# Written order for VectorE and ScalarE in attention, and the later modulation rows summed on VectorE

## Chip, cores and metric

One core of one Trainium2 chip. The metric is the time of one execution of the program on the device, in microseconds (us): the median of three runs before the change. Times of single instructions and waits come from one profiled execution. TensorE does the matrix products and the transposes (into PSUM), VectorE, ScalarE and GpSimd the elementwise work, SyncE issues the DMA loads and stores.

## What is computed

One layer of a diffusion backbone over 1024 latent tokens of width 1024, with 256 context tokens. Cut to what matters here (`mod` is one product of a 1024-vector with a 1024 x 6144 matrix, which gives six rows of 1024):

```python
mod = jax.nn.silu(c) @ w_ada + b_ada
sh1, sc1, gt1, sh2, sc2, gt2 = jnp.split(mod, 6, axis=-1)
h = modulate(rmsnorm(x, g_mix), sh1, sc1)          # h * (1 + scale) + shift
q, k, v, bg, cg, hv = jnp.split(h @ w_in, SPLIT_POINTS, axis=-1)
att = windowed_attention(rope(q), rope(k), v, k_c, v_c, sink)   # 8 heads of 64, window of 128
conv = bg * conv3(cg * hv)                          # depthwise, 3 taps
x = x + gt1 * (jnp.concatenate([att, conv], -1) @ w_out)
h2 = modulate(rmsnorm(x, g_ffn), sh2, sc2)
x = x + gt2 * expert_choice_ffn(h2, w_router, w_gate, w_up, w_down)   # 16 experts
return rmsnorm(x, g_final)
```

The softmax of a query runs over a sink, the 256 context keys and the latent keys within 128 positions. The inputs are float32; every large operand is split into a high and a low half in a reduced format, and a product is three products of halves.

## The kernel before, in words

The work is staged. First come sh1 and sc1 by themselves (to 37.9 us), since everything else needs them. Then x and ctx are normed, transposed, modulated and split into hT, and the keys and values are projected (`build_hT`, `proj_kv`, driven by `kv_stream`, to 90.8). `q_stream` projects eight query tiles of 128 tokens (`q_proj`: 24 matmuls of 512 columns, rotary on VectorE at L327 to L334, the split into halves at L509 and L510; `q_turn` transposes them, L520). Beside both runs `mod_stream`: the other four modulation rows. For each it loads 8 pieces of 512 KB (L460), ScalarE scales a piece by silu(c) (L461) and GpSimd adds it (L463); a small product with 0/1 columns sums over the partitions (L473), the bias is added (L489) and the rows go to DRAM (`rows_d`), from where later stages fetch them. A function `weave` draws from both generators in proportion to given totals, which sets the order in which instructions are written; `urgent` gives the projection's a higher priority with the scheduler.

Attention is 32 units, eight blocks of 128 queries times four head pairs. `scores(u)` makes the two score blocks of a pair on TensorE (L563, L565), adds the mask and takes the row maximum (L575), negates and scales it (L577), and has ScalarE form the exponentials with their sums (L578). Two additions and an exponential of the sink complete the sum (L585 to L587), a reciprocal follows (L588), and the blocks are scaled by it, one on ScalarE (L592), one on VectorE (L594). `values(u)` transposes the probabilities (L622) in three groups, ScalarE casts each group to its high half (L625), VectorE subtracts for the low half (L626, here called pth), TensorE forms the value products (L613), and the two parts are joined into attT (L639, L643). In the loop of `attention` the scores of unit u and the values of unit u-1 alternate, and `weave` mixes in `conv`: 12 weight tiles (`wcs`: loaded, cast on ScalarE at L710, low half on GpSimd at L711), each 16 steps of three matmuls (L730 to L732). After every third tile's partner the three taps of the conv are applied: GpSimd at L755 and L760, ScalarE at L759. `prepare` and what follows it loads the output projection's weights in four parts, multiplies them by gt1 (L776) and splits them (L223, L224). Then `project` runs over the token tiles with the router and the sort, and the experts follow.

Only TensorE runs in written order (`manual_schedule`); the other engines' instructions are put in order by a scheduler. Large tiles come from 21 slots, small ones from rings of three buffers (`w4`, `wm`).

## Time and profile before

| | us |
|---|---|
| runs of the kernel, median (lowest to highest) | 1165.14 (1164.18 to 1167.07) |
| profiled execution, its own time | 1163.48 |
| its span | 1161.7 |
| busy: TensorE, VectorE, ScalarE, GpSimd | 1058.4, 967.2, 766.1, 351.0 |
| to the end of sh1 and sc1 | 37.9 |
| hT, keys and values | 37.9 to 90.8 |
| queries | 90.8 to 178.5 |
| attention and conv | 178.5 to 433.5 |
| output projection, router, sort | 433.5 to 576.4 |
| experts | 576.4 to 1126.0 |
| last rows out | 1126.0 to 1161.7 |

The stretches are cut where the first instruction of the next stage's kind starts on TensorE. Busy time is the time in which an engine executes instructions; matmuls overlap in the engine's pipeline, so a busy TensorE need not be at its peak. In a row of waits the engine and line on the left had nothing to do until the one on the right finished.

### The profile page before, as it was taken

Reading aid. Unit: us, or ns where it says so; the run is one execution under the profiler, and the core shown is the slowest. Engines: PE = TensorE matmul, PEld = TensorE weight load, DVE = VectorE, ACT = ScalarE, POOL = GpSimd, SP = SyncE. Lnnn points to the kernel's source line nnn. Section 1 sums busy time; section 2 is a strip of 40 time slices with the busy share of each in tenths; the row PEclk is TensorE's granted clock in tenths of the full one; section 3 lists DMA queues with packets and bytes.
Section 4 is the critical chain, followed back from the end, with each engine's and each line's share of the span. In section 5 each row is a group of like instructions: output and inputs, shape, how many; then the busy total and the mean of one; then the engine's idle time right before and its main releaser. Section 6 shows DMA issues by size and latency. Waiting matters only on the chain.

```text
span 1161.7 us, 15615 instructions
## 1 busy us (share of the span) xinstructions
PE 1058.4 (91%) x5486; PEld 873.5 (75%) x5486; DVE 967.2 (83%) x1661; ACT 766.1 (66%) x1058; POOL 351.0 (30%) x292
## 2 busy tenths in 40 slices
PE   6786889999899998999399999999999999999981
PEld 2675667888788877888288888888888888888861
DVE  7888455887878785389899999999999999999975
ACT  7565655767666643232288878878878877888853
POOL 0457681221303031222212433322333322330022
PEclk9897999999999999999599999999999999999996
DMA  9644440010101079648789999999999999999555
GB/s 376 232 164 144 164 146 19 24 33 1 55 1 37 19 278 339 181 127 270 273 322 356 399 403 390 391 388 389 395 404 392 389 389 389 394 404 390 203 195 221
DMA packets 90790, 292.89 MB, mean 252 GB/s; under 512 B 7044, under 2 KB 20816, under 8 KB 89688
## 3 DMA queue, kind: packets, MB, share of 16 engines
q1 hardware_dynamic: 84808, 270.40, 61.0%
q0 software_dynamic: 5904, 21.50, 7.7%
q8 instruction: 43, 0.70, 0.2%
q14 instruction: 35, 0.29, 0.1%
HBM read 266.69 MB, written 25.18 MB: 251 GB/s over the span
## 4 chain that ended last, share of the span: by engine, by line
PE 72%; DVE 13%; issue 5%; ACT 4%; DMA 4%; POOL 1%; POOLq 0%; ACTq 0%; DVEq 0%; SPq 0%
PE pg L1313 14%; PE pu L1313 14%; PE py L1313 13%; PE po L879 7%; PE ps_cv L731 3%; PE ps_cv L730 3%; PE ps_cv L732 3%; PE pt L622 2%; PE po_att L613 2%; DVE whl L1150 2%; PE ps_s L565 2%; PE xTp L1299 1%; PE ps_s L563 1%; PE pl L954 1%; PE hTtp L1299 1%
## 5 line engine op out<-in xcount | busy, mean ns | idle before, releaser
L1150 DVE TENSOR_TENSOR whl<-raw,whl 128x1024 fp32r<-128x1024 f32 x384 | 455.2, 1224 | 29.9 <-ACT whl L1147 18.9
L1147 ACT CAST whl<-raw 128x1024 fp32r<-128x1024 f32 x384 | 400.2, 1054 | 100.2 <-PE pu L1313 35.6
L1313 PE MATMUL pg<-whl,xT 128*128 128x512 f32 x768 | 186.2, 395 | 2.1 <-DVE whl L1150 2.1
L1313 PE MATMUL pu<-whl,xT 128*128 128x512 f32 x768 | 180.9, 392 | 0.0
L1313 PEld LDWEIGHTS pg<-whl,xT 128*128 128x128 f32 x768 | 142.3, 189 | 31.6 <-DVE whl L1150 2.9
L1313 PE MATMUL py<-whl,hTt 128*128 128x512 f32 x720 | 165.9, 389 | 0.0
L1313 PEld LDWEIGHTS pu<-whl,xT 128*128 128x128 f32 x768 | 143.0, 188 | 29.4
L1313 PEld LDWEIGHTS py<-whl,hTt 128*128 128x128 f32 x720 | 135.1, 188 | 28.4 <-DVE whl L1150 0.3
L1278 POOL TENSOR_SCALAR oh<-iota,pos 128x128 bf16<-128x128 f32 x104 | 100.5, 981 | 0.5
L1371 POOL DMA_INDIRECT acc_d<-yt,idx x15 | 38.5, 2565 | 196.0 <-DVE yt L1359 196.0
L1323 POOL DMA_INDIRECT xr<-h_d,idx x16 | 22.3, 1395 | 199.2 <-DVE gate_w L1289 199.2
L730 PE MATMUL ps_cv<-hTh,wcs 128*128 128x512 f32 x192 | 81.5, 424 | 0.0
L463 POOL TENSOR_TENSOR acc<-acc,wmod 128x1024 f32<-128x1024 f32 x28 | 70.0, 2518 | 27.8 <-ACT wmod L461 26.7
L625 ACT CAST pth<-pt 128x512 fp32r<-128x512 f32 (+1 forms) x88 | 46.1, 524 | 46.2 <-PE pt L622 46.1
L731 PE MATMUL ps_cv<-hTl,wcs 128*128 128x512 f32 x192 | 76.1, 397 | 0.0
L732 PE MATMUL ps_cv<-hTh,wcs 128*128 128x512 f32 x192 | 76.0, 396 | 0.0
L879 PE MATMUL po<-woh,ah 128*128 128x512 f32 x240 | 70.8, 404 | 0.6 <-ACT woh L223 0.6
L626 DVE TENSOR_TENSOR pth<-pt,pth 128x512 fp32r<-128x512 f32 (+1 forms) x88 | 53.9, 613 | 20.1 <-ACT pth L625 19.2
L711 POOL TENSOR_TENSOR wcs<-wcr,wcs 128x1024 fp32r<-128x1024 f32 x12 | 28.6, 2389 | 110.2 <-ACT wcs L710 87.5
L578 ACT ACTIVATE sm<-sm,negm 128x640 f32<-128x640 f32 (+1 forms) x64 | 51.6, 807 | 4.0 <-DVE negm L577 3.9
L575 DVE CUSTOM_DVE_ANT_0 sm<-ps_s,maskt,sink 128x640 f32<-128x640 f32 (+1 forms) x56 | 48.3, 863 | 6.9 <-PE ps_s L565 6.3
L879 PEld LDWEIGHTS po<-woh,ah 128*128 128x128 f32 x240 | 44.1, 191 | 9.4 <-ACT woh L223 1.0
(297 smaller groups left out, 1828.4 us busy)
## 6 DMA issues: line engine op xcount, KB each, us to landing
raw<-in_w_gate_dram SPq DMA_DIRECT2D x64, 1024.0 KB, 9.6
raw<-in_w_up_dram SPq DMA_DIRECT2D x64, 1024.0 KB, 7.8
raw<-in_w_down_dram SPq DMA_DIRECT2D x64, 1024.0 KB, 9.6
wmod<-in_w_ada_dram SPq DMA_DIRECT2D x32, 512.0 KB, 3.7
wa<-in_w_ada_dram SPq DMA_DIRECT2D x8, 1024.0 KB, 5.3
wcr<-in_w_in_dram SPq DMA_DIRECT2D x12, 512.0 KB, 3.8
xt<-in_x_dram SPq DMA_DIRECT2D x4, 1024.0 KB, 20.6
wor<-in_w_out_dram SPq DMA_DIRECT2D x4, 1024.0 KB
```

Of the source, the lines that this page charges most:

```text
L463: nc.gpsimd.tensor_tensor(acc, acc, wt, op=OP.add)
L575: nc.vector.tensor_tensor_reduce(dst, src, mk, op0=OP.add, op1=OP.max, scale=1.0, scalar=sink8[:, h:h + 1], accum_out=mx[:, b, h:h + 1])
L578: nc.scalar.activation(sm, sm, AF.Exp, bias=negm[:, b, h:h + 1], scale=0.125, accum_out=esum[:, b, h:h + 1])
L626: nc.vector.tensor_tensor(pth[:, 1, :n], pt[:, :n], pth[:, 0, :n].bitcast(F32), op=OP.subtract)
L730: mm(ps, wsp[:, 0, k], hi, start=k == 0, stop=False)
L731: mm(ps, wsp[:, 0, k], lo, start=False, stop=False)
L732: mm(ps, wsp[:, 1, k], hi, start=False, stop=k == KC - 1)
L879: mm(po[n], a, wo[k // 4, n][j][:, k % 4], start=first, stop=last)
L1147: nc.scalar.copy(w[:, 0], t[:, k % 2])
L1150: low = nc.vector.tensor_tensor(w[:, 1], t[:, k % 2], w[:, 0].bitcast(F32), op=OP.subtract)
L1278: nc.gpsimd.tensor_scalar(oh[:, t], iota1, pos[:, t, 0, e:e + 1], None, op0=OP.is_equal)
L1313: mm(ps[n], a_hl[:, a, k], w[:, j, n * 512:(n + 1) * 512], start=first, stop=last)
```

## The change

Six things, in the order of the program:

1. Small constants: all rows of `b_ada` and `g_ffn` are loaded and transposed with the others, so that a modulation row can be finished as a column (`modv`, 128 x 32).
2. `build_hT` gives all steps the same engines: ScalarE modulates, ScalarE casts, VectorE subtracts. The low half of the k/v weights goes from GpSimd to VectorE.
3. `mod_stream` and `urgent` go. Rows 1 and 2 (sh2, sc2) are summed on VectorE, one 128x1024 chunk of each per query tile, tied behind that tile's split (`mod_tile`); row 0 (gt1) is done in attention, one step a unit, in chunks of 384, 384 and 256 columns (`mod_attention`); row 3 (gt2) in 16 steps beside the projection of tiles 1 to 4 (`last_row`). Sums over partitions are small products with a column of ones.
4. The query halves are made with the factor -0.125, the masks are positive, and a minimum takes the maximum's place: it is then directly the bias of the exponential, which runs with scale -1 over one more column, that of the sink. The `negm` instructions and the sink's two additions and exponential go; a copy of two sink values a unit comes.
5. Attention and conv run in written order on VectorE and ScalarE too. The loop has six explicit places a unit; the join of a unit's values moves into the next unit; the second exponential has a place of its own.
6. Conv weights' low halves and the taps go from GpSimd to VectorE, in pieces of 512 columns at set steps; the first tap goes to ScalarE. Loading, gating and splitting of the output weights stand apart.

```diff
-        nc.gpsimd.tensor_tensor(wkv_l[:, ks], wkv_r[:, ks], wkv_h[:, ks].bitcast(F32), op=OP.subtract)
+        nc.vector.tensor_tensor(wkv_l[:, ks], wkv_r[:, ks], wkv_h[:, ks].bitcast(F32), op=OP.subtract)
...
-        if k % 2:
-            nc.scalar.activation(hf, ps[:, :n], AF.Identity, scale=mscale[:, k, j:j + 1], bias=mshift[:, k, j:j + 1])
-            nc.vector.tensor_copy(hi, hf)
-            nc.vector.tensor_tensor(lo, hf, hi.bitcast(F32), op=OP.subtract)
-        else:
-            nc.vector.tensor_scalar(hf, ps[:, :n], mscale[:, k, j:j + 1], mshift[:, k, j:j + 1],
-                                    op0=OP.mult, op1=OP.add)
-            nc.scalar.copy(hi, hf)
-            (nc.gpsimd if mem is None or k < 4 else nc.vector).tensor_tensor(lo, hf, hi.bitcast(F32), op=OP.subtract)
+        nc.scalar.activation(hf, ps[:, :n], AF.Identity, scale=mscale[:, k, j:j + 1], bias=mshift[:, k, j:j + 1])
+        nc.scalar.copy(hi, hf)
+        nc.vector.tensor_tensor(lo, hf, hi.bitcast(F32), op=OP.subtract)
...
-            nc.sync.dma_start(wt, wada_k[k][:, (2 + r) * D:(3 + r) * D])
-            nc.scalar.activation(wt if k else acc, wt, AF.Copy, scale=silu_c[:, k:k + 1])
-            if k:
-                nc.gpsimd.tensor_tensor(acc, acc, wt, op=OP.add)
...
+    def mod_add(src, k, acc, out=None):
+        if k == 0:
+            return nc.vector.tensor_scalar(acc, src, silu_c[:, 0:1], None, op0=OP.mult)
+        return nc.vector.scalar_tensor_tensor(acc if out is None else out, src, silu_c[:, k:k + 1], acc, op0=OP.mult,
+                                              op1=OP.add)
...
+    def mod_tile(t):
+        if t == 0:
+            macc.extend(slots.get((2, D), F32, "acc"))
+        st_ = [wm("wmod") for _ in range(2)]
+        for r in (1, 2):
+            mod_load(st_[r - 1], r, t, slice(0, D))
+        yield
+        for r in (1, 2):
+            add = mod_add(st_[r - 1], t, macc[0][:, r - 1])
+            tc.add_manual_dep(add.ins, q_split[-1].ins.name,
+                              mybir.DependencyInfo(mybir.DependencyClass.Sync, mybir.DependencyReason.DATA),
+                              reason="order")
...
+            w = cols[n].stop - cols[n].start
+            src = stage[:, i % 2, :w]
+            last = k == KC - 1
+            mod_add(src, k, accp[:, :w], src if last else None)
+            if last:
+                yield 1
+                mod_sums(accp, src, 0, cols[n].start // 128)
+            load(i + 2)
...
         qs = w4("qs", (8, 2, HD), F32R)
         tv = t1.rearrange("p (h d) -> p h d", d=HD)
-        nc.scalar.copy(qs[:, :, 0, :], tv)
-        nc.vector.tensor_tensor(qs[:, :, 1, :], tv, qs[:, :, 0, :].bitcast(F32), op=OP.subtract)
+        nc.scalar.activation(qs[:, :, 0, :], tv, AF.Copy, scale=-0.125)
+        low = nc.vector.scalar_tensor_tensor(qs[:, :, 1, :], tv, -0.125, qs[:, :, 0, :].bitcast(F32), op0=OP.mult,
+                                       op1=OP.subtract)
         qs_of[t] = qs
+        q_split.append(low)
+        for _ in mt:
+            pass
...
-    weave([(urgent(steps(kv_stream(), q_stream())), 95.0), (mod_stream(), 56.0)])
+    for _ in steps(kv_stream(), q_stream()):
+        pass
...
+        def exp(i):
+            h = 2 * hp + i
+            sx = sm2[:, i, :W + 1]
+            nc.scalar.activation(sx, sx, AF.Exp, bias=mx[:, b, h:h + 1], scale=-1.0,
+                                 accum_out=esum[:, b, h:h + 1])
...
             else:
                 mk = maskt[:, 0:W]
-            nc.vector.tensor_tensor_reduce(dst, src, mk, op0=OP.add, op1=OP.max, scale=1.0,
+            if i == 0:
+                nc.vector.tensor_copy(sm2[:, :, W], sink8[:, hs])
+                for f in joined[:1]:
+                    f(0)
+            nc.vector.tensor_tensor_reduce(dst, src, mk, op0=OP.add, op1=OP.min, scale=1.0,
                                            scalar=sink8[:, h:h + 1], accum_out=mx[:, b, h:h + 1])
-            nc.vector.tensor_scalar(negm[:, b, h:h + 1], mx[:, b, h:h + 1], -0.125, None, op0=OP.mult)
-            nc.scalar.activation(sm, sm, AF.Exp, bias=negm[:, b, h:h + 1], scale=0.125,
-                                 accum_out=esum[:, b, h:h + 1])
             if i == 0:
-                yield
-        hs = slice(2 * hp, 2 * hp + 2)
-        r = rec[:, b, hs]
-        nc.vector.tensor_tensor(r, sinkb[:, hs], negm[:, b, hs], op=OP.add)
-        nc.scalar.activation(r, r, AF.Exp)
-        nc.vector.tensor_tensor(r, r, esum[:, b, hs], op=OP.add)
-        nc.vector.reciprocal(r, r)
+                exp(0)
+                if joined:
+                    joined.pop()(1)
+            yield
+        exp(1)
+        yield
+        nc.vector.reciprocal(rec[:, b, hs], esum[:, b, hs])
...
-            for i, g in enumerate((sc, va, sc, va, va, va)):
-                next(g, None)
-                if i < 5:
-                    yield 1
-                if u == 0 and g is sc:
-                    yield 1
+            next(sc, None)
+            if u == 4 * NT:
+                joined[0](0)
+                joined.pop()(1)
+            if u and mrow is not None:
+                next(mrow, None)
+            yield 1
+            next(va, None)
+            yield 1
+            next(sc, None)
+            yield 1
+            next(va, None)
+            next(sc, None)
+            yield 1
+            if u == 0:
+                yield 1
+            next(va, None)
+            next(sc, None)
+            yield 1
+            next(va, None)
+        joined[0](0)
+        joined.pop()(1)
...
+    def conv_split(i, low, n):
+        if i < 12:
+            raw, wsp, _ = conv_w_of[i]
+            ks = slice(4 * n, 4 * n + 4)
+            if low:
+                nc.vector.tensor_tensor(wsp[:, 1, ks], raw[:, ks], wsp[:, 0, ks].bitcast(F32), op=OP.subtract)
+            else:
+                nc.scalar.copy(wsp[:, 0, ks], raw[:, ks])
...
+                    at = 8 * half + k
+                    if at in (7, 8, 9, 10):
+                        conv_split(i + 1, *divmod(at - 7, 2))
+                    if part == 2 and at < 4:
+                        j, n0 = 1 + at // 2, at % 2 * 512
+                        yt_ = st["y"][:, n0:n0 + 512]
+                        nc.vector.scalar_tensor_tensor(yt_, st["u"][:, j + n0:j + n0 + 512],
+                                                       convT_w[:, 4 * j + f:4 * j + f + 1], yt_, op0=OP.mult, op1=OP.add)
+                    if k < KC - 1:
+                        yield 1
...
-                nc.gpsimd.tensor_scalar(y, u[:, 0:S], convT_w[:, f:f + 1], None, op0=OP.mult)
-                tap = wm("tap", (S,))
-                for j in (1, 2):
-                    w = convT_w[:, 4 * j + f:4 * j + f + 1]
-                    nc.scalar.activation(tap, u[:, j:j + S], AF.Copy, scale=w)
-                    nc.gpsimd.tensor_tensor(y, y, tap, op=OP.add)
+                nc.scalar.activation(y, st["u"][:, 0:S], AF.Copy, scale=convT_w[:, f:f + 1])
                 st["y"] = y
...
-    weave([(steps(attention(), prepare()), 160.0), (conv(), 161.0)])
...
+    pb = p2(1, "po_att")
+    with tc.manual_schedule(engines={ET.PE, ET.DVE, ET.Activation}):
+        weave([(steps(attention(), prepare()), 152.0), (conv(), 161.0)])
...
+        yield 6
+        for i, (n, k) in enumerate(items):
+            mod_add(mem[:, 1 + i % 3], k, mem[:, 0])
+            load(i + 3)
+            if k == KC - 1:
+                yield 1
+                mod_sums(p1(1, "prow"), mem[:, 0], 3, 4 * n)
+            yield 1.8
+        mod_row(p1(1, "prow"), 3)
+        slots.put(s_)
```

Where it moves instructions, at three places. Names in the rows: t is a query tile under rotary, qs its halves, wmod a loaded piece of a modulation row, acc its sum; ISA is the masked minimum or maximum with its read-out (mx), pth a low half of transposed probabilities, wcr and wcs a conv weight and its halves, attT the joined values, stage and po_att the pieces and the running sum of the gt1 row.

VectorE, query stage, from the rotary of one tile to the start of the next, before:

```order
L327 TENSOR_TENSOR t_1281<-ps_q,ropet 128x512
L329 TENSOR_TENSOR t_1281<-ps_q,ropet 128x512
L333 TENSOR_TENSOR t_1281<-t_1281 128x8x32
L334 TENSOR_TENSOR t_1281<-t_1281 128x8x32
L510 TENSOR_TENSOR qs<-t_1281,qs 128x8x64
L327 TENSOR_TENSOR t_1340<-ps_q,ropet 128x512
L329 TENSOR_TENSOR t_1340<-ps_q,ropet 128x512
```

and with the change:

```order
L322 TENSOR_TENSOR t_1246<-ps_q,ropet 128x512
L324 TENSOR_TENSOR t_1246<-ps_q,ropet 128x512
L328 TENSOR_TENSOR t_1246<-t_1246 128x8x32
L329 TENSOR_TENSOR t_1246<-t_1246 128x8x32
L624 COPY sm_1321<-sink_282 128x2
L545 SCALAR_TENSOR_TENSOR qs<-t_1246,qs 128x8x64
L447 SCALAR_TENSOR_TENSOR acc_860<-wmod,silu_c,acc_860 128x1024 x2
L322 TENSOR_TENSOR t_1298<-ps_q,ropet 128x512
L324 TENSOR_TENSOR t_1298<-ps_q,ropet 128x512
```

The two chunks (L447 x2) now stand between a tile's split and the next tile's rotary.

VectorE, attention, a unit in which a conv weight is split, from the first pth of the values to the scaling of the scores, before:

```order
L626 TENSOR_TENSOR pth<-pt,pth 128x512
L575 ISA sm_2238,mx<-ps_s,maskt,sink_285 128x640
L575 ISA mx 128x1
L577 TENSOR_SCALAR negm<-mx 128x1
L585 TENSOR_TENSOR rec<-sinkb,negm 128x2
L626 TENSOR_TENSOR pth<-pt,pth 128x512
L587 TENSOR_TENSOR rec<-rec,esum 128x2
L588 RECIPROCAL rec<-rec 128x2
L626 TENSOR_TENSOR pth<-pt,pth 128x256
L594 TENSOR_SCALAR sm_2238<-sm_2238,rec 128x640
```

and with the change (from the join of the last unit's values on):

```order
L698 TENSOR_TENSOR attT_1487<-po_att,up 64x128 x2
L447 SCALAR_TENSOR_TENSOR po_att<-stage,silu_c,po_att 128x384
L828 TENSOR_TENSOR cg<-ps_cv,cg 128x512
L676 TENSOR_TENSOR pth<-pt,pth 128x512
L627 ISA sm_1840,mx<-ps_s,maskt,sink_282 128x640
L627 ISA mx 128x1
L781 TENSOR_TENSOR wcs_1750<-wcr,wcs_1750 128x512
L676 TENSOR_TENSOR pth<-pt,pth 128x512
L781 TENSOR_TENSOR wcs_1750<-wcr,wcs_1750 128x512
L676 TENSOR_TENSOR pth<-pt,pth 128x256
L636 RECIPROCAL rec<-esum 128x2
L642 TENSOR_SCALAR sm_1840<-sm_1840,rec 128x640
```

The L577, L585 and L587 rows are gone; the join, a chunk and two halves of a conv weight's low part (L781) stand among the rest, the first of them ahead of the second pth, the second ahead of the third.

VectorE, from the last query tile into attention, before:

```order
L327 TENSOR_TENSOR t_1386<-ps_q,ropet 128x512
L329 TENSOR_TENSOR t_1386<-ps_q,ropet 128x512
L333 TENSOR_TENSOR t_1386<-t_1386 128x8x32
L334 TENSOR_TENSOR t_1386<-t_1386 128x8x32
L855 MEMSET vals 128x512
L510 TENSOR_TENSOR qs<-t_1386,qs 128x8x64
L489 TENSOR_TENSOR bias<-mrows,bias 4x1024
L575 ISA sm_1404,mx<-ps_s,maskt,sink_285 128x512
L575 ISA mx 128x1
```

and with the change:

```order
L322 TENSOR_TENSOR t_1298<-ps_q,ropet 128x512
L324 TENSOR_TENSOR t_1298<-ps_q,ropet 128x512
L627 ISA sm_1321,mx<-ps_s,maskt,sink_282 128x512
L627 ISA mx 128x1
L328 TENSOR_TENSOR t_1298<-t_1298 128x8x32
L329 TENSOR_TENSOR t_1298<-t_1298 128x8x32
L545 SCALAR_TENSOR_TENSOR qs<-t_1298,qs 128x8x64
L781 TENSOR_TENSOR wcs_1313<-wcr,wcs_1313 128x512
L447 SCALAR_TENSOR_TENSOR acc_860<-wmod,silu_c,acc_860 128x1024 x2
L781 TENSOR_TENSOR wcs_1313<-wcr,wcs_1313 128x512
```

The bias of the rows is gone; the first minimum of attention stands ahead of the second half of the last rotary, and the first conv weight's low halves stand behind the last split, on either side of the last two chunks.

## Rows read from the trace of the kernel before

**Rows 1.** The table of stretches of the core, one row each (bounds in us from the start of the span, length, busy us of each engine with its number of instructions, granted TensorE clock as a share of full speed, share of the DMA engines, GB/s): the query stage, attention, and the output projection with the router.

```profile
90.80:178.50 87.70, 68.10 (x300) 50.44 (x298) 55.51 (x78) 46.60 (x65) 63.75 (x38) 0.92 0.47 150
178.50:433.50 255.00, 247.71 (x1465) 213.10 (x1466) 197.76 (x509) 164.93 (x345) 56.56 (x23) 0.99 0.15 50
433.50:576.40 142.90, 118.57 (x654) 99.87 (x652) 105.77 (x440) 43.09 (x91) 32.09 (x64) 0.91 0.74 238
```

**Rows 2.** Waits in the query stage (engine and line, what it waited for, us in total, times, longest us).

```profile
DVE t L327 <- PE ps_q L503: 24.6, 7, 6.0
PE pq L520 <- DVE qs L510: 13.1, 5, 4.6
```

**Rows 3.** All instructions of one line over the whole span (number, duration in ns as minimum/median/maximum, first and last start in us, forms): the split of a query tile, and the add of a softmax sum.

```profile
L510 DVE TENSOR_TENSOR qs<-t,qs x8: 691/692/2106, 113.6 to 176.6; 128x512 fp32r<-128x512 f32 x8
...
L587 DVE TENSOR_TENSOR rec<-rec,esum x32: 142/160/2326, 186.0 to 409.8; 128x2 f32<-128x2 f32 x32
```

**Rows 4.** Groups of instructions in the query stage (line, engine, operation, names, shapes, number | busy us, mean ns of one | idle time of the engine before them, and what ended it): GpSimd's additions of the modulation, and ScalarE's cast of a query tile.

```profile
L463 POOL TENSOR_TENSOR acc<-acc,wmod 128x1024 f32<-128x1024 f32 x24 | 59.5, 2496 | 25.7 <-ACT wmod L461 24.5 <-PE ps_q L503 0.5 <-ACT vx L343 0.5
...
L509 ACT CAST qs<-t 128x512 fp32r<-128x512 f32 x8 | 5.0, 622 | 18.9 <-DVE t L334 18.9
```

**Rows 5.** Groups in attention, the same columns; pth is a transposed probability block, sm a score block, rec the reciprocal sums, attT the joined output, wcs a split conv weight.

```profile
L626 DVE TENSOR_TENSOR pth<-pt,pth 128x512 fp32r<-128x512 f32 x64 | 44.1, 690 | 19.4 <-ACT pth L625 18.5
L575 DVE CUSTOM_DVE_ANT_0 sm<-ps_s,maskt,sink 128x640 f32<-128x640 f32 x48 | 42.4, 882 | 5.0 <-PE ps_s L565 4.4
...
L711 POOL TENSOR_TENSOR wcs<-wcr,wcs 128x1024 fp32r<-128x1024 f32 x10 | 23.9, 2392 | 107.9 <-ACT wcs L710 85.2 <-PE po_att L613 22.7
...
L643 DVE TENSOR_TENSOR attT<-po_att,up 64x128 f32<-64x128 f32 x64 | 18.1, 282 | 10.8 <-ACT up L639 10.4
...
L594 DVE TENSOR_SCALAR sm<-sm,rec 128x640 f32<-128x640 f32 x24 | 13.6, 568 | 0.2
...
L587 DVE TENSOR_TENSOR rec<-rec,esum 128x2 f32<-128x2 f32 x32 | 12.0, 376 | 5.2 <-ACT rec L586 4.5
...
L626 DVE TENSOR_TENSOR pth<-pt,pth 128x256 fp32r<-128x256 f32 x24 | 9.8, 409 | 0.7 <-ACT pth L625 0.7
...
L575 DVE DVE_READ_ACCUMULATOR2_ANT mx<- 128x1 f32 x64 | 5.3, 83 | 0.0
```

**Rows 6.** Time line of TensorE in the query stage (start us, us, engine, line, operation, names, shapes, number, and in brackets the idle time before it with what ended it): first and last of 24 products between two turns, a turn, the next product.

```profile
154.50 0.48 PE L501 MATMUL ps_q<-wqh,hTh 128*128 128x512 f32 x1
...
159.84 0.39 PE L503 MATMUL ps_q<-wqh,hTl 128*128 128x512 f32 x1
162.81 1.09 PE L520 MATMUL pq<-ident,qs 128*128 128x128 f32 x8 [2.59 <-DVE qs L510]
163.66 0.48 PE L501 MATMUL ps_q<-wqh,hTh 128*128 128x512 f32 x1
```

**Rows 7.** Groups in the k/v stage (columns as in rows 4): products with the low half of hT, GpSimd's low half, and ScalarE's modulation.

```profile
L318 PE MATMUL ps_kv<-wkvh,hTl 128*128 128x256 f32 x64 | 20.0, 312 | 4.8 <-POOL hTl L297 2.5 <-DVE hTl L292 2.3
...
L297 POOL TENSOR_TENSOR hTl<-hf,hTh 128x512 fp32r<-128x512 f32 x4 | 5.7, 1436 | 6.0 <-ACT hTh L296 6.0
...
L290 ACT ACTIVATE hfs<-ps_xt,mshift,mscale 128x512 f32<-128x512 f32 x4 | 3.1, 776 | 0.0
```

**Rows 8.** All instructions of a line (columns as in rows 3): two forms of VectorE that multiply by a scalar and combine with a second tensor, in later stages.

```profile
L933 DVE SCALAR_TENSOR_TENSOR h<-xres,rstd,rowsA x7: 1283/1285/1286, 453.9 to 536.6; 128x1024 f32<-128x1024 f32 x7
...
L1359 DVE SCALAR_TENSOR_TENSOR yt<-py,gate_w,GT x32: 739/744/752, 622.9 to 1145.8; 128x512 f32<-128x512 f32 x32
```

**Rows 9.** Time line between the query stage and attention (columns as in rows 6): the row sums of the modulation, and the first score products.

```profile
172.71 3.60 PE L473 MATMUL mrows<-acc,sel 128*4 128x512 f32 x8
...
178.47 0.73 PE L563 MATMUL ps_s<-kcv,qT 128*128 128x256 f32 x2 [2.16 <-DVE bias L489]
```

**Rows 10.** Time line in attention (columns as in rows 6): the first score product of four units, and one add of a softmax sum.

```profile
291.70 2.33 DVE L587 TENSOR_TENSOR rec<-rec,esum 128x2 f32<-128x2 f32 x1
...
292.06 0.40 PE L563 MATMUL ps_s<-kcv,qT 128*128 128x256 f32 x2
...
301.64 0.40 PE L563 MATMUL ps_s<-kcv,qT 128*128 128x256 f32 x2
...
308.59 0.40 PE L563 MATMUL ps_s<-kcv,qT 128*128 128x256 f32 x2
...
403.99 0.40 PE L563 MATMUL ps_s<-kcv,qT 128*128 128x256 f32 x2
```

**Rows 11.** Waits of TensorE in attention (columns as in rows 2).

```profile
PE po_att L613 <- DVE pth L626: 5.1, 8, 1.1
...
PE pt L622 <- DVE sm L594: 1.9, 2, 1.5
```

**Rows 12.** The chain of waits at the end of attention, in order of time (start us, us, what).

```profile
408.13 5.34 DMA rowsA<-rows_d
...
425.71 5.48 DMA wor<-in_w_out_dram
431.38 6.68 DVE wor L776 x2
```

**Rows 13.** DMA issues on the page (tile, tensor, queue, number, KB each, median us from issue to landing).

```profile
wmod<-in_w_ada_dram SPq DMA_DIRECT2D x32, 512.0 KB, 3.7
```

More of the change, by code (lines that the diff above doesn't have):

```diff
@@ new lines, in tile_layer, with mod_sums @@
+    modv = consts.tile([128, 32], F32, name="modv")
+    def mod_add(src, k, acc, out=None):
[3 more added lines that the diff above has]
+                                              op1=OP.add)
+    def mod_sums(pr, acc, r, k0=0):
+        n = acc.shape[1] // 128
+        for q in range(n):
+            mm(pr[:, q:q + 1], acc[:, q * 128:(q + 1) * 128], ones_f, start=True, stop=True)
+        c = 8 * r + k0
+        v = modv[:, c:c + n]
+        nc.vector.tensor_tensor(v, pr[:, 0:n], badaT[:, c:c + n], op=OP.add)
+        if r == 2:
+            nc.vector.scalar_tensor_tensor(v, v, 1.0, gffnT[:, k0:k0 + n], op0=OP.add, op1=OP.mult)
@@ new lines, in mod_end, with mod_attention, load @@
+    def mod_end():
+        pr = p2(0, "prow")
+        for r in (1, 2):
+            mod_sums(pr[:, r - 1], macc[0][:, r - 1], r)
+        slots.put(macc[1])
+        for r in (1, 2):
+            mod_row(pr[:, r - 1], r)
+    def mod_attention(accp):
+        stage = work.tile([128, 2, 384], F32, tag="early", name="stage")
+        cols = (slice(0, 384), slice(384, 768), slice(768, 1024))
+        items = [(n, k) for n in range(3) for k in range(KC)]
+        def load(i):
+            if i < len(items):
+                n, k = items[i]
+                w = cols[n].stop - cols[n].start
+                mod_load(stage[:, i % 2, :w], 0, k, cols[n])
+        load(0)
+        load(1)
+        yield 1
+        for i, (n, k) in enumerate(items):
+            w = cols[n].stop - cols[n].start
+            src = stage[:, i % 2, :w]
[5 more added lines that the diff above has]
+            load(i + 2)
+            yield 1
+        mod_row(p1(3, "prow"), 0)
@@ L634, in values, with join @@
             flush()
-        if b // 4 not in attT:
-            attT[b // 4] = slots.get((4, 512), F32, "attT")
-        up = work.tile([64, 2, 128], F32, tag="up", name="up")
-        nc.scalar.copy(up.rearrange("p b c -> p (b c)"), po[64:128])
-        pov = po.rearrange("p (b c) -> p b c", b=2)
-        for par in range(2):
-            dst = attT[b // 4][0][64 * par:64 * par + 64, hp, (b % 4) * 128:(b % 4 + 1) * 128]
-            nc.vector.tensor_tensor(dst, pov[:64, par], up[:, par], op=OP.add)
-        if b % 2 and hp == 3:
-            slots.put(qT[b // 2][1])
+        def join(step):
+            if step == 0:
+                up_of[0] = work.tile([64, 2, 128], F32, tag="up", name="up")
+                nc.scalar.copy(up_of[0].rearrange("p b c -> p (b c)"), po[64:128])
+                return
+            if b // 4 not in attT:
+                attT[b // 4] = slots.get((4, 512), F32, "attT")
+            up = up_of[0]
+            pov = po.rearrange("p (b c) -> p b c", b=2)
+            for par in range(2):
+                dst = attT[b // 4][0][64 * par:64 * par + 64, hp, (b % 4) * 128:(b % 4 + 1) * 128]
+                nc.vector.tensor_tensor(dst, pov[:64, par], up[:, par], op=OP.add)
+            if b % 2 and hp == 3:
+                slots.put(qT[b // 2][1])
+        joined.append(join)
     rt = {}
@@ L1191, in before, with last_row_part @@
         return steps(*side)
+    def last_row_part():
+        c = 0.0
+        while c < 10:
+            w = next(lrow)
+            c += w
+            yield w
     def once(f, *args):
```

182 lines of the change are left out of this document (85 added, 97 removed).

## Prediction, made before the changed kernel was run

> **What bounds the kernel now.** I read the table of stretches first, since no engine is the bound for the whole span. In attention (178.5 to 433.5) TensorE is busy 247.71 of 255.0 us; in the query stage (90.8 to 178.5) no engine is busier than 68.10 of 87.7 [rows 1]. So the query stage is bound by a chain, and the waits say by which: VectorE waits 24.6 us for TensorE's query sums and TensorE 13.1 us for VectorE's split, by turns, while GpSimd adds up modulation rows [rows 2]. The third view, durations of one line, shows why: the same 128x512 split takes 691 or 2106 ns, and an add over 128x2 elements 160 or 2326 ns [rows 3]. GpSimd's 128x1024 additions take 2496 ns each [rows 4], and the long cases are of that size. Instructions with an operand in PSUM keep to their time, 690 ns in the mean of 64 [rows 5]. So a VectorE instruction with two SBUF inputs is held behind GpSimd's. The chain of waits of the query stage confirms what is late: the split, by 2.59 us in the tile shown [rows 6].
>
> **A. K/v stage.** The three steps from PSUM to the two halves of hT now run as ScalarE, ScalarE, VectorE for every k; GpSimd's low halves (1436 ns each, with 2.5 us of TensorE waiting for them and 2.3 for VectorE's) go [rows 7]. ScalarE pays 0.78 for the modulation [rows 7] and 0.62 for a cast of 128x512 [rows 4], 1.4 a step, against TensorE's 1.8 (four transposes at 0.106 and twelve 256-column products at 0.116, half of a 512-column one; both from [rows 6]): hidden, in the two feeds of x. Waits removed: 2.5 + 2.3, and VectorE instructions held by GpSimd; new: two low halves of the k/v weights, 128x1024, which VectorE does in about 1.2 each (an estimate from the 1285 of a like form [rows 8]) ahead of the products. **-4**, from -7 to -1.
>
> **B. Query stage.** Between two turns the 24 matmuls of a tile's worth start at 154.50 to 159.84, 23 intervals of 0.232; with the turn (0.85 between pq at 162.81 and the next matmul at 163.66) a tile is 6.4 us of TensorE [rows 6]. From the end of k/v (90.8) the eight tiles then cost 8 x 24 x 0.23 = 44.2, seven turns 6.0, the 32 transposes of the keys 3.4, and one wait of about 5 at the start for the keys' rotary and the first split: 58.6, against 81.8 now (to the row sums at 172.7 [rows 9]). VectorE's part of a tile, unheld, is 2 x 0.69 + 2 x 0.41 for the rotary (by instructions of those sizes [rows 5]), 0.62 of waiting for ScalarE [rows 4], 0.74 for the split, and two chunks of 1.28: a 128x1024 form with a scalar took 1285 ns, the 512 form 744 [rows 8]. That is 6.1 us, just under TensorE's 6.4. The chunks stand behind the split in the order, so they delay only the next tile's rotary. Their loads go one pair a tile, 1 MB in 6.4 us or 164 GB/s, and the stage moves 150 now [rows 1]. **-23**; -26 if the wait at the start is covered, -17 if a tile is 7.1.
>
> **C. From queries to attention.** The 3.60 us of row sums on TensorE and the 2.16 of waiting for their bias go [rows 9]. In their place the first conv weight's low half, once GpSimd's, stands on VectorE behind the last rotary, the first minimum and the last split (1.38 + 0.83 + 0.82 + 0.62 + 0.74 + 0.69 = 5.1 after the last query product). **-1**, from -3 to +2.
>
> **D. Attention.** This term decides. Taken from VectorE: four tiny instructions a unit, of which the add over 128x2 took 376 ns in the mean [rows 5] and 160 undisturbed [rows 3]; with 0.16 to 0.38 for each, 20 to 48 us in all, and I take 31. Put on it: a copy a unit (about 0.1), one chunk a unit in 24 units (0.4 to 0.74), conv low halves (20 x 0.69, once 10 x 2392 ns of GpSimd), and taps (4 x 0.744 for each of three f): about 42 [rows 5, 8]. The total goes from 197.76 to about 209 of 255 [rows 1].
>
> The rule that speaks for no loss, first by the row: TensorE is busy 97% of this stretch, VectorE 78, so 57 us of VectorE stand idle [rows 1]. The Trainium skill (Perfetto Trace Analysis, "Identifying the Most-Contended Engine") says to optimise the engine of highest occupancy; read that way, work put on VectorE costs nothing while it stays under TensorE, and the stalls that GpSimd causes go. By it the term would be about -7: of the present loss of 12 (below) what the first unit and the end cost would stay. The rows do not let me take that whole: a unit is 6.95 us from first score product to the next (301.64 to 308.59), but the unit from 292.06 to 301.64 took 9.6, after one 128x2 add of 2.33 us held the chain [rows 10], and transposes waited up to 1.5 for the scaling behind it [rows 11]. One late instruction costs; the mean does not show it.
>
> So I count by unit. Now: 32 units begin, the first at 178.47 [rows 9], the last at 403.99 [rows 10]; that is 225.5 us for 31 units, 10 more than 31 x 6.95, and I put 2 on the end, where conv runs out alone: 12. Then, in a written order, where VectorE and ScalarE no longer pass a late instruction:
> - Ten units with a conv split. VectorE: minima 2 x (0.88 + 0.08), joins 0.56, chunk 0.57, three pth 0.69 + 0.69 + 0.41, two low halves 1.38, reciprocal 0.17, scaling 0.57, copy 0.1: 7.1 against 6.95 [rows 5]. The lower bound is 0.15 each; the upper is 1.45, if the low half ahead of the second pth (it is written there) holds the last value product. I take 0.9: **9**.
> - Three tap passes: 2.98 more over two units, with 1.25 of room in each: 0.5 to 3, taken 2: **6**.
> - Some 17 plain units, VectorE 5.7: 0 to 0.3 (the third pth stands behind the second exponential), taken 0.2: **3**.
> - One unit in which conv waits for a free slot: **3**; first unit, and the 24 small products and three transposes of the rows: **4**.
>
> Sum 25, against 12: **+13**; lower end -7, upper +23 (all upper values, 35).
>
> **E. Into the output projection.** The chain there is now a row's load 5.34, a gate, a weight's load 5.48, two gates 6.68, and splits [rows 12]. The row of gt1 is ready earlier and the loads are issued apart from the gates, which helps; the gates now stand in VectorE's written order among taps. **+2**, from -4 to +6.
>
> **F. Projection.** Sixteen 128x512 steps (16 x 0.744 = 11.9 on VectorE [rows 8]) and 4 MB of loads beside it. VectorE is busy 105.77 of 142.9 [rows 1], so most is covered; if not, all 11.9 in the worst place. **+1**, up to +6.
>
> **Sum.** -4 - 23 - 1 + 13 + 2 + 1 = -12 from the profiled execution's 1163.5, or 1151.5. The median of the runs is 1165.1, 1.7 more: **1153**.
>
> **Rivals.** *Attention loses nothing* (D at -7): GpSimd's lock is gone, and units run at TensorE's pace. For it: 57 us of idle VectorE, and only two waits of TensorE that name VectorE, 5.1 and 1.9 [rows 11]. Against it: the sum of 7.1 for a unit with a split. It gives 1153 - 20 = 1133. This is what the Trainium skill's rule above would make of it. *Every unit becomes as long as one with a split* (slower): the chain of minimum 1, exponential 1, cast, third pth, value product is strictly ordered, and each unit costs 1.45 more if the third pth ends later than TensorE's next scores even without a low half; 33 x 1.45 = 48 in place of 25 gives 1153 + 23 = 1176. The kernel is slower than before from 1.1 us a unit on all 33: the 12 lost now and the 25 that the other terms bring, by 33. For it: ScalarE's exponential and cast lie in series with VectorE's work in that chain. Against: in a plain unit VectorE has 1.25 us to spare. *The chunks hold the rotary* in the query stage: if their loads land late, each tile's next rotary waits; 2 us a tile, 16 in all, gives 1169. Against: loads of this size land in 3.7 us [rows 13], and the second of a tile is issued as soon as the first chunk of the tile before has freed a buffer, a tile's 6.4 ahead.
>
> **Chances.** Forecast 0.58 (its own range 1143 to 1163), attention without loss 0.24, chunks holding 0.08, every unit long 0.10. A measurement of this kernel tells a change of over 0.3%, 3.5 us: 1161.6 to 1168.6 is "same". Of the forecast's 0.58, 0.03 lies there; of the chunks' case 0.04; the rest of it and the long units are slower. Faster 0.55 + 0.24 = 0.79, same 0.07, slower 0.14. The range takes in the forecast's own and most of the first rival, and leaves out the long units and half of the chunks' case: 1130 to 1167.
>
> **What would show it.** In the profile after: in the query stage the split at 0.74 in every tile and a tile every 6.4 us (B right); GpSimd idle in attention and no 128x2 instruction over 0.2 us; waits of TensorE's value products for VectorE's pth in the ten split units of about 1 us (D right), near none (first rival), or in all units (second). Query tiles at over 8 us with VectorE waiting for a DMA would be the third. The prediction is wrong if attention takes under 250 or over 285 us, or the query stage over 72.

## The result, and the profile after

The changed kernel takes 1158.2 us (median; 1157.0 to 1164.8) against 1165.8 of before on the same chip: a ratio of 0.9946, interval 0.9921 to 0.9970. Timed once more it was 0.9940 (0.9920 to 0.9959). So 7.5 us were gained where 12 were forecast. Its two profiled executions took 1164.8 and 1163.3, longer than its median; the terms below are read from both, and what differs between them is part of the finding. Against the 1163.5 of the profiled execution before they are 1.3 longer and 0.2 shorter, so the differences of the table do not add up to the 7.5. An execution nearer the median is that of the experiment on the old step in hT (1156.8): it has 275.3 for D, 135.3 for F and 583.5 in the last row.

| stretch, by TensorE's products | before | changed | again | difference | forecast |
|---|---|---|---|---|---|
| start to last k/v product (A) | 90.8 | 85.8 | 84.7 | -5.0, -6.1 | -4 |
| to last query product (B) | 81.6 | 55.2 | 55.2 | -26.4 | -23 |
| to first conv product (C) | 7.1 | 6.1 | 5.8 | -1.0, -1.3 | -1 |
| to last conv product (D) | 254.0 | 279.2 | 275.4 | +25.2, +21.4 | +13 |
| first 30 output products (E) | 10.8 | 15.3 | 15.3 | +4.5 | +2 |
| to the first expert product (F) | 131.9 | 138.0 | 136.2 | +6.1, +4.3 | +1 |
| from there to the end | 585.3 | 583.2 | 588.7 | -2.1, +3.4 | 0 |

The query stage, attention and the output projection in the first profile (columns as in [rows 1]; the cuts lie where these stages now begin):

```profile
85.80:141.20 55.40, 53.78 (x283) 45.24 (x282) 44.40 (x84) 20.25 (x40) 0.00 (x0) 1.00 0.35 115
141.20:426.40 285.20, 265.37 (x1516) 227.06 (x1515) 203.66 (x486) 162.75 (x326) 2.24 (x13) 0.95 0.20 65
426.40:579.80 153.40, 123.84 (x672) 102.95 (x670) 118.72 (x461) 44.77 (x93) 32.78 (x63) 0.89 0.76 245
```

TensorE is now busy 97% of the query stage, 78% before. Attention is 30 us longer, five of them ahead of its first conv product, and its granted clock fell from 0.99 to 0.95. Its 285.2 us are just past the 285 that the prediction named as a sign of being wrong; the second profile has 281.2 here. The waits of the query stage, against [rows 2]:

```profile
DVE t L322 <- PE ps_q L537: 4.3, 6, 1.9
```

VectorE's wait for the sums fell from 24.6 to 4.3. The split, the chunks, the conv halves and the taps in all their executions (columns as in [rows 3]):

```profile
L545 DVE SCALAR_TENSOR_TENSOR qs<-t,qs x8: 691/692/693, 98.2 to 144.8; 128x512 fp32r<-128x512 f32 x8
...
L447 DVE SCALAR_TENSOR_TENSOR acc<-wmod,silu_c,acc x14: 1277/1282/1285, 105.3 to 148.8; 128x1024 f32<-128x1024 f32 x14
...
L781 DVE TENSOR_TENSOR wcs<-wcr,wcs x24: 679/683/693, 147.0 to 411.9; 128x512 fp32r<-128x512 f32 x24
...
L814 DVE SCALAR_TENSOR_TENSOR cg<-u,smallT,cg x16: 741/747/754, 200.3 to 424.9; 128x512 f32<-128x512 f32 x16
```

The split never takes 2.1 us any more, and the prices taken from [rows 8] hold. Two turns of the query stage, against [rows 6]: 138.97 less 132.62 is the 6.4 of a tile, with no idle time in brackets.

```profile
132.62 1.03 PE L559 MATMUL pq<-ident,qs 128*128 128x128 f32 x8
133.41 0.48 PE L535 MATMUL ps_q<-wqh,hTh 128*128 128x512 f32 x1
...
138.97 1.03 PE L559 MATMUL pq<-ident,qs 128*128 128x128 f32 x8
```

From the queries to attention, against [rows 9], and then the sums of sh2 and sc2 in front of the scores of unit 2:

```profile
141.23 0.40 PE L610 MATMUL ps_s<-kcv,qT 128*128 128x256 f32 x2
...
147.06 0.80 PE L804 MATMUL ps_cv<-hTh,wcs 128*128 128x512 f32 x1 [5.20 <-ACT wcs L783]
...
160.99 1.04 PE L559 MATMUL pq<-ident,qs 128*128 128x128 f32 x8
161.86 1.84 PE L454 MATMUL prow<-ones_f,acc 128*128 128x1 f32 x16
163.96 3.10 PE L454 MATMUL prow<-ones_f,acc 128*128 128x1 f32 x16 [0.26 <-DVE modv L457]
167.32 0.38 PE L463 MATMUL prow<-ident,modv 128*8 128x128 f32 x1 [0.26 <-DVE modv L457]
168.04 0.38 PE L463 MATMUL prow<-ident,modv 128*8 128x128 f32 x1 [0.34 <-ACT prow L465]
168.76 0.80 PE L610 MATMUL ps_s<-kcv,qT 128*128 128x256 f32 x2 [0.34 <-ACT prow L465]
```

TensorE spends 161.86 to 168.76, 6.9 us, on the sums: it is busy 5.7 of them, with products that have one column and two small transposes, and waits 1.2 for their results (in brackets), since the chain product, addition, transpose, copy stands in its order as one block. After it the score products take 0.80 instead of 0.40: the clock is at the lower of its two levels (granted 0.50 from 168.76 to 172.00). The waits of TensorE in attention, against [rows 11], from 220 us on:

```profile
PE po_att L454 <- DVE attT L698: 4.6, 3, 1.6
PE po_att L663 <- DVE pth L676: 2.6, 8, 0.8
PE ps_s L610 <- DVE mx L627: 1.9, 3, 0.9
```

The value products, on which D was worked out, wait less than before: over the whole of attention 3.5 us, against 5.1. New are three waits of the sums of gt1 (L454) for the join of the last unit's values (L698), which the change has moved into this unit. One of them lies in unit 10, which begins with the first line; the line at 235.57 is its second score block, and the last line begins unit 11:

```profile
229.38 0.40 PE L610 MATMUL ps_s<-kcv,qT 128*128 128x256 f32 x2
...
231.70 0.80 PE L454 MATMUL po_att<-ones_f,stage 128*128 128x1 f32 x6 [1.57 <-DVE attT L698]
235.57 0.63 PE L610 MATMUL ps_s<-kcv,qT 128*128 128x256 f32 x2
240.36 0.40 PE L610 MATMUL ps_s<-kcv,qT 128*128 128x256 f32 x2
```

The unit takes 11.0 us in place of 6.95. The chain at the end of attention, against [rows 12], has no DMA in it any more, but the gates (L859) and splits (L224, L225) of the output weights, most of them on VectorE, one behind the other:

```profile
418.41 2.29 DVE wor L859
420.73 1.92 ACT woh L224
422.68 1.89 DVE wol L225
...
440.76 7.55 PE po L968 x32
```

### The profile page after: what moved, and what is told of

The parts are those of the page before. It is cut to its first block, busy times and chain, and to the rows that moved or that the text cites. A ratio compares the mean times of both kernels' runs of the same rounds, so it can differ in the third digit from the quotient of the medians.

```text
span 1163.0 us, 15584 instructions
## 1 busy us (share of the span) xinstructions
PE 1063.8 (91%) x5537; PEld 884.5 (76%) x5537; DVE 955.4 (82%) x1648; ACT 743.1 (64%) x1030; POOL 204.8 (18%) x228
## 4 chain that ended last, share of the span: by engine, by line
PE 72%; DVE 13%; DMA 4%; ACT 3%; issue 2%; POOL 0%; POOLq 0%; ACTq 0%; DVEq 0%; SPq 0%
PE pg L1438 14%; PE pu L1438 14%; PE py L1438 13%; PE po L968 5%; PE ps_cv L804 3%; PE ps_cv L805 3%; PE ps_cv L806 3%; PE po_att L663 2%; PE pt L672 2%; DVE pth L676 2%; DVE whl L1239 2%; DMA gt<-in_w_ada_dram 2%; PE ps_s L612 1%; DVE sm L627 1%; PE xTp L1424 1%
## 5 line engine op out<-in xcount | busy, mean ns | idle before, releaser
L804 PE MATMUL ps_cv<-hTh,wcs 128*128 128x512 f32 x192 | 83.7, 436 | 5.2 <-ACT wcs L783 5.2
L602 ACT ACTIVATE sm<-sm,mx 128x641 f32<-128x641 f32 (+1 forms) x64 | 51.7, 808 | 40.9 <-DVE mx L627 40.9
L806 PE MATMUL ps_cv<-hTh,wcs 128*128 128x512 f32 x192 | 77.8, 405 | 0.0
L1496 POOL DMA_INDIRECT acc_d<-yt,idx x15 | 38.5, 2566 | 195.7 <-DVE yt L1484 195.7
L627 DVE CUSTOM_DVE_ANT_0 sm<-ps_s,maskt,sink 128x640 f32<-128x640 f32 (+1 forms) x56 | 48.2, 860 | 10.8 <-PE ps_s L612 10.7
L672 PEld LDWEIGHTS pt<-ident,sm 128*128 128x128 f32 x304 | 39.8, 145 | 15.9 <-DVE pth L676 1.7
L672 PE MATMUL pt<-ident,sm 128*128 128x128 f32 x304 | 49.3, 279 | 2.5 <-ACT prow L465 1.2
```

The source lines that it names most:

```text
L602: nc.scalar.activation(sx, sx, AF.Exp, bias=mx[:, b, h:h + 1], scale=-1.0, accum_out=esum[:, b, h:h + 1])
L627: nc.vector.tensor_tensor_reduce(dst, src, mk, op0=OP.add, op1=OP.min, scale=1.0, scalar=sink8[:, h:h + 1], accum_out=mx[:, b, h:h + 1])
L672: nc.tensor.transpose(pt[:, (2 * q + i) * 128:(2 * q + i + 1) * 128], sm2[:, i, j * 128:(j + 1) * 128], ident)
L804: mm(ps, wsp[:, 0, k], hi, start=k == 0, stop=False)
L806: mm(ps, wsp[:, 1, k], hi, start=False, stop=k == KC - 1)
```

## Experiments

The unit lengths below are between first score products; "excess" is what a unit has over 6.95, corrected by 0.69 for each conv step that it has more or fewer than five. In the first and the last four units, whose score blocks are narrower, 6.25 stands for 6.95 (before the change units 29 and 30 took 6.24 and 6.25).

**The changed kernel again** (no edit).

> The changed kernel itself once more. Its profiled execution took 1164.8, the other five 1157.0 to 1160.0, so this one shows where 7 us differ between executions of one program. Both theories: about 1158, with unit lengths in attention as in the first profile (31 units in 259 us, 33 more than before) and the same long units 0 to 2, 10, 19 and 28; the 7 us should then be missing in the output projection (139 us from its first dense products to the experts, against 133 before).

1158.6 (1156.3 to 1163.4). The 7 us lie in no single place: against the first profile, D was 3.8 shorter and F 1.8, while the last stretch was 5.5 longer. In D, units 10, 21 and 28 are 1.6 shorter each, unit 19 is 1.6 longer, and units 1 and 2 are 1.6 shorter together. Unit 10 of this execution:

```profile
227.33 0.40 PE L610 MATMUL ps_s<-kcv,qT 128*128 128x256 f32 x2
...
229.65 0.80 PE L454 MATMUL po_att<-ones_f,stage 128*128 128x1 f32 x6 [1.57 <-DVE attT L698]
232.23 0.39 PE L610 MATMUL ps_s<-kcv,qT 128*128 128x256 f32 x2
236.74 0.40 PE L610 MATMUL ps_s<-kcv,qT 128*128 128x256 f32 x2
```

The wait is the same 1.57 us, the unit 9.4. The granted clock of the 4 us behind the products (columns as in [rows 1]) was 0.73 in the first profile and 1.00 here:

```profile
234.00:238.00 4.00, 4.00 (x19) 3.49 (x18) 1.58 (x3) 0.82 (x2) 0.00 (x0) 0.73 0.08 30
```

```profile
232.00:236.00 4.00, 4.00 (x25) 3.50 (x24) 2.39 (x5) 1.99 (x5) 0.00 (x0) 1.00 0.06 22
```

So whether such a wait costs the clock too differs between executions of one program. The last part was stretched in one place: GpSimd's last indirect store of expert outputs (L1496) took 11.38 us here and 5.70 in the first profile. Why it did stays open.

```profile
1107.00 11.38 POOL L1496 DMA_INDIRECT acc_d<-yt,idx  x1 [30.28 <-DVE yt L1484]
```

```profile
1113.66 5.70 POOL L1496 DMA_INDIRECT acc_d<-yt,idx  x1 [30.28 <-DVE yt L1484]
```

**Sums at the end of a unit.**

```diff
             next(va, None)
+            if now == 2:
+                kind = next(mrow, None)      # sums and transpose of gt1
+            if u:
+                next(mend, None)             # unit 1: all 16 products; units 2, 3: a transpose each
...
```

> The partition sums of the modulation rows in attention are placed at the end of a unit, behind its last value product, and those of sh2 and sc2 are taken in one go at the end of unit 1 with one transpose each in units 2 and 3, where the changed kernel does all of it ahead of unit 2's scores. Theory 1 (the loss in attention is TensorE waiting in written order beside these tiny products: units 1, 2, 10, 11, 19, 28 and 29 are 24 us longer than 6.95 each, 1.4 of it also before): 10 to 16 us faster than the changed kernel, 1143 to 1148. Theory 2 (the loss is VectorE's added work and the written order of VectorE and ScalarE): at most 4 us faster, 1154 to 1158.

1148.4 (1145.5 to 1148.8), 10 us under the changed kernel: theory 1, at the edge of its range. D was 263.5. Units 10, 19 and 28 have an excess of 0.6 to 0.8, where the changed kernel has 2.5 to 4.1. Unit 10's products no longer wait, and the next scores follow in 0.6:

```profile
230.42 0.72 PE L454 MATMUL po_att<-ones_f,stage 128*128 128x1 f32 x6
231.01 0.48 PE L614 MATMUL ps_s<-kcv,qT 128*128 128x256 f32 x2
```

**Without the sums.** The rows of gt1, sh2 and sc2 get no sum and no transpose; gt2, summed beside the projection, keeps both.

```diff
-            mm(pr[:, q:q + 1], acc[:, q * 128:(q + 1) * 128], ones_f, start=True, stop=True)
-        nc.vector.tensor_tensor(v, pr[:, 0:n], badaT[:, c:c + n], op=OP.add)
+        nc.vector.tensor_tensor(v, acc[:, 0:n], badaT[:, c:c + n], op=OP.add)
...
-        nc.tensor.transpose(pr[:8, :128], modv[:, 8 * r:8 * r + 8], ident)
...
```

> The partition sums of gt1, sh2 and sc2 (24 small products) and their three transposes are left out of attention; the sums over k on VectorE stay, and a copy of the wrong column takes each sum's place, so the rows are not the modulation. Theory 1 (these products in TensorE's order are most of the loss): units 1, 2, 10, 11, 19, 28 and 29 at 6.95 but for what unit 1 had before (0.8), and 15 to 20 us faster than the changed kernel, 1138 to 1143. Theory 2 (the written order and VectorE's added work): at most 6 faster.

1143.3 (1142.8 to 1145.0), 15 under the changed kernel: theory 1. D was 256.8, 2.8 above before. The 2.8 is a balance: the excess of units 4 to 27 sums to 14.6, against 10.4 before, so what the splits, the taps, the written order and the unit without conv cost is little more than the stalls of before that went. The 24 products with their three transposes, their waits and the clock behind them come to 18.6 of the second profile's 275.4 (22.4 of the first's 279.2). Unit 1 keeps an excess of 1.3, units 10 and 19 none. D of the second profile, of the sums at the end of a unit, and of this run (columns as in [rows 1]):

```profile
145.71:421.08 275.37, 260.74 (x1511) 223.06 (x1512) 200.02 (x479) 159.92 (x321) 2.24 (x13) 0.97 0.19 62
```

```profile
145.61:409.08 263.47, 255.79 (x1511) 220.43 (x1511) 199.41 (x478) 159.81 (x321) 2.24 (x13) 0.99 0.20 64
```

```profile
145.44:402.23 256.79, 249.09 (x1459) 214.07 (x1460) 199.61 (x479) 159.76 (x324) 2.24 (x13) 0.99 0.21 66
```

TensorE is idle 14.6, 7.7 and 7.7 us. So at the end of a unit the products cost 6.7 us of TensorE and no waiting, and some 12 of the 18.6 hang on their place.

**Written order for TensorE alone.**

```diff
-    with tc.manual_schedule(engines={ET.PE, ET.DVE, ET.Activation}):
+    with tc.manual_schedule(engines={ET.PE}):
```

> Only TensorE in written order in attention; VectorE and ScalarE are ordered by the scheduler, as before the change, all else as changed. Theory 1: the written order costs nothing in the plain units (3 to 5, 13, 15, 18, 22 and 24 have 6.95 or less), so this is no faster: 0 to +8, 1158 to 1166. Theory 2 (the order holds the queues): 8 to 15 faster, 1143 to 1150.

1153.5 (1152.1 to 1154.9), 5 faster: between the two, and theory 1 as I put it was wrong on this. In the profile the units with taps and a split fall from an excess of 1.7, 1.7 and 2.2 to 0.8, 0.8 and 1.1; most plain units rise from 0 to between 0.2 and 0.6. So the written order costs about 1 us in a unit with late work on VectorE and saves a little in the others.

**Conv halves on GpSimd.**

```diff
-                nc.vector.tensor_tensor(wsp[:, 1, ks], raw[:, ks], wsp[:, 0, ks].bitcast(F32), op=OP.subtract)
+                nc.gpsimd.tensor_tensor(wsp[:, 1, ks], raw[:, ks], wsp[:, 0, ks].bitcast(F32), op=OP.subtract)
```

> The conv weights' low halves go back to GpSimd, in the same two pieces at the same steps; the written order of VectorE and ScalarE stays. If GpSimd's lock costs more than VectorE's added work: units with a split get longer than the present 0.75 of excess, by 0.5 to 1.5 in ten units, and the time is 3 to 10 slower, 1161 to 1168. Rival (VectorE's place in the written order is what these units lose): their excess goes to under 0.3 and the time is 3 to 7 faster, 1151 to 1155.

1158.4 (1156.3 to 1161.3): no difference, and neither expectation. Units 7, 14 and 17 fell from 0.75 to 0.3, so VectorE's place in the order does cost them 0.45; the units with taps did not change, and the sum is too small to see in the time. That GpSimd holds VectorE's two-input instructions costs nothing that the time shows here. A likely reason, not tested: there are two halves of 1.3 us in a unit with a split, and hardly a small two-input instruction is left beside them.

**The first conv weight's load earlier.**

```diff
+        if t == 7:
+            early_w.append(wm("wcr", (8, 128)))
+            nc.sync.dma_start(early_w[0], win_v[:, :, CG0:CG0 + 128])
         mt = mod_tile(t)
...
```

> The load of the first conv weight is issued ahead of the last query tile's two modulation pieces instead of behind them. If the 5.2 us that TensorE waits for its cast are the load's (issued at 141.2, behind pieces that wait for buffers): first conv product within 1 us of the first scores (5.5 now) and 4 to 6 us faster, 1152 to 1155. Rival: the low half behind the last split holds it (the prediction's account): first conv product still 4 to 5 us behind the scores, no more than 1 us faster.

1155.6 (1153.2 to 1157.7), 3 faster. The first conv product started 0.47 behind the first scores:

```profile
141.62 0.40 PE L614 MATMUL ps_s<-kcv,qT 128*128 128x256 f32 x2
...
142.09 0.40 PE L811 MATMUL ps_cv<-hTh,wcs 128*128 128x512 f32 x1
```

So the load was late, not the low half: in the changed kernel it is issued at 141.17, behind the last pieces of the modulation, which wait for a buffer. Of the 5.1 us won there, 2 did not reach the time: units 1 and 2 are 0.8 longer than in the second profile, and the k/v stage, which lies ahead of the edit's place, was 1.5 longer.

**Chunks on GpSimd.**

```diff
-            add = mod_add(st_[r - 1], t, macc[0][:, r - 1])
+            nc.scalar.activation(wt if t else acc, wt, AF.Copy, scale=silu_c[:, t:t + 1])
+            if t:
+                nc.gpsimd.tensor_tensor(acc, acc, wt, op=OP.add)
...
```

> The chunks of sh2 and sc2 in the query stage go back to ScalarE's scaling and GpSimd's addition, one pair a tile, all else as changed. If GpSimd's additions hold VectorE's two-input instructions (theory 1): splits of a query tile at up to 2 us again, query stage 62 to 72 us (55.2 changed, 81.6 before), time 7 to 15 slower, 1165 to 1173. Rival: the stage is bound by TensorE at 6.4 a tile and half as many additions as before fit beside it: at most 58 us, at most 3 slower.

1172.6 (1166.0 to 1175.1), 14 slower: theory 1. The query stage is 71.5, and the longest split is long again:

```profile
L545 DVE SCALAR_TENSOR_TENSOR qs<-t,qs x8: 689/693/2829, 107.4 to 160.7; 128x512 fp32r<-128x512 f32 x8
```

Of B's 26.4 us, 16.3 hang on the engines that scale and add the chunks, with the same loads at the same places; the edit also drops the tie of a chunk to its tile's split, and what each part does was not tried alone. The other 10 may go with two rows here in place of four, which was not tried either. Five of the 16.3 come back behind the stage, where the first conv product follows the last query product in 0.7.

**The old step in hT.**

```diff
-        nc.scalar.activation(hf, ps[:, :n], AF.Identity, scale=..., bias=...)
-        nc.scalar.copy(hi, hf)
+        if k % 2:                                 # as before the change
...
+            (nc.gpsimd if mem is None or k < 4 else nc.vector).tensor_tensor(lo, hf, hi.bitcast(F32), op=OP.subtract)
```

> The step from PSUM to the halves of hT as before the change (VectorE and ScalarE by turns, some low halves on GpSimd), all else as changed. If the even split of engines is what ended the k/v stage 5 to 6 us earlier (84.7 to 85.8, 90.8 before): last k/v product at 89 to 91, time 3 to 6 slower, 1161 to 1164. Rival: the stage gained because GpSimd's additions and ScalarE's scaling of modulation rows left it: last k/v product before 87, at most 2 slower.

1158.3 (1156.8 to 1158.6), last k/v product at 83.9: the rival. The split of engines gained nothing that shows.

**Before, with the modulation stream later.**

```diff
     def mod_stream():
-        yield 18
+        yield 28
```

> The kernel before the change, with the stream of the later modulation rows started later (its first yield 28 instead of 18), so that nearly all of its scaling on ScalarE and its additions on GpSimd lie behind the k/v stage. If it was that stream, not the split of engines in the building of hT, which held the k/v stage: last k/v product at 84 to 87 (90.8 before, 84 to 86 changed). The query stage then takes as much longer as the additions are pushed into it, 82 to 92, so the time is 0 to 6 slower than before. Rival: the last k/v product stays at 89 to 91, and what the change gained there is something else.

1166.0 (1162.1 to 1167.6), no different from before; the last k/v product is at 83.2, 90.8 before (columns as in [rows 3]):

```profile
L318 PE MATMUL ps_kv<-wkvh,hTl x64: 278/283/388, 52.4 to 83.2; 128*128 128x256 f32 x64
```

```profile
L318 PE MATMUL ps_kv<-wkvh,hTl x64: 278/283/580, 52.3 to 90.8; 128*128 128x256 f32 x64
```

So it was the stream that held the k/v stage, by 7.6 us; what was won there was lost again between the last query product and the first conv product (16.4, 7.1 before).

**Most of the last row left out.** 14 of the 16 pieces of gt2 are not loaded and not added.

```diff
-        items = [(n, k) for n in range(2) for k in range(KC)]
+        items = [(n, 0) for n in range(2)]
...
```

> Of the last modulation row, beside the projection, 14 of the 16 pieces are left out (loads and additions, so the row is not the full sum). If these 11 us of VectorE and 3.7 MB are what makes the projection longer: 4 to 6 us faster, 1152 to 1154. If they are hidden, as predicted: 0 to 2 faster.

1156.0 (1154.0 to 1159.7), about 2.5 faster, between the two expectations and with times that overlap those of the changed kernel. F was 132.8, against 136.2 and 138.0; but in the other profiles with all sixteen steps F lies anywhere from 133.2 (conv halves on GpSimd) to 138.5 (without the sums), with 135.6 in the middle. So the steps are mostly hidden, some 3 us show, and one profile cannot give that figure closely.

**Both corrections, and both without the written order.**

> The two corrections together: sums at the end of units (10 faster alone) and the first conv weight's load ahead of the last pieces (3 faster alone). If they are independent waits: 1143.5 to 1146. If the second only moves TensorE to the next wait in unit 1: 1147 to 1149.

> The same, with only TensorE in written order in attention (5 faster alone). If the scheduler's order gains in the units with splits and taps, as in the profile of that run (0.4 to 1.1 in each of ten), it adds to the others: 1138 to 1142. If its gain was the same waits that the moved sums took away: 1143 to 1146.

1143.8 (1143.0 to 1147.6), a ratio of 0.9824 (0.9805 to 0.9842) to before, and 1144.2 (1142.6 to 1145.4). The two corrections add up. Leaving the order of VectorE and ScalarE to the scheduler then gains nothing more: units with taps are shorter and plain units longer, as above, but unit 1 has an excess of 11.5 (7.1 in the other). Why it grew there I did not follow.

## Why the prediction was half right

- **A** was right in size by luck, and wrong in cause. The stage did get 5 to 6 us shorter, but not by the new step in hT: the old step gives the same, and before, with the stream of modulation rows moved out, the stage ends at 83.2.
- **B** was right: VectorE's two-input instructions were held by GpSimd, a tile is TensorE's 6.4, and the chunks fit. The start covered itself, so the result is the -26 that stood as the other end. (The 81.8 of the stage before is 81.9 by its two rows, which changes nothing.)
- **C** was right in size only, by luck too. What TensorE waited for is a load behind other loads in SyncE's order; I had followed the low half on VectorE and not the queue.
- **D** is the step that failed, in its last item: "first unit, and the 24 small products and three transposes of the rows: 4". Measured, the products, their waits and the clock behind them are 18.6 (second profile): TensorE is busy 11.7 longer, 7.2 of it with the products and transposes themselves, and idle 6.9 longer; the granted clock of D is 0.97 with them and 0.99 without. The 4 has no working; the products' own time alone is more, and I did not count that they are links of a chain in TensorE's written order, nor that a stall there can take the clock to the lower level. The other items were too high: the plain units lose nothing (0.2 each was taken), the splits and taps 9.5 by excess in place of 15, although the four taps of a pass fall into one unit (6, 16 and 25) and not over two. That value products would wait for VectorE about 1 us in each of the ten split units was wrong: it is 3.5 us in 11 waits.
- The rule that work on VectorE costs nothing while TensorE is busier gave -7 for D. It misses by far with the sums, and by ten without them (+2.8).
- **E** and **F** were small and both too low. E: VectorE is busy 14.6 of the 15.3 us, with gates, splits and taps, and was busy all of the 10.8 before; that its work sets the length was read from this and not tested. F: some 3 of the row's 11.9 us show, where 1 was taken and 6 was the bound; the rest of the 4 to 6 lies within what differs between executions.

None of the rivals came about. In all, A to C gained 32 to 34 us where 28 were expected, and D to F lost 30 to 36 where 16 were expected.

## What to carry to other kernels

Price tiny instructions by their number and their place, not only by the length of one: here 24 one-column products and three transposes were 7 us by themselves and 18.6 in their place. In a written order, a product that needs another engine's result, or whose result goes through another engine and back, holds the whole queue meanwhile, and it belongs where its inputs are long done and its result is not wanted soon. When an engine's lock is the suspect, compare the shortest and the longest time of one instruction, and see whether what the longest has over is within the length of one of the other engine's. A load that must be early has to be issued early, so read the queue that issues it, and not only who computes on it.

## What was not expected

The same wait of 1.57 us in the same unit cost 2.5 us in one execution and 4.0 in another, with a granted clock of 1.00 and of 0.73 behind it. Two executions of one program can therefore differ by some 4 us in a stage whose instructions all have the same order and the same waits: D was 279.2 and 275.4, and in two other runs with this attention 279.1 (most of the last row left out) and 275.3 (the old step in hT).
